# Squared-ReLU MLP of an encoder layer: the place of one PSUM copy on ScalarE, and the order of GpSimd's DMAs

## The chip, the cores and the metric

The kernel runs on one core of one Trainium2 chip. A core has engines that each work through their own list of instructions in order: TensorE (PE in the profile; its weight loads are listed apart as PEld), VectorE (DVE), ScalarE (ACT), GpSimd (POOL) and SyncE (SP). SP and GpSimd issue the transfers (DMAs) here. The engines meet through semaphores. TensorE writes PSUM, which is cut into banks of 128 rows by 512 floats.

The metric is the device time of one execution in microseconds (us), as the median of three runs. Beside it stands one execution with the profiler on, from which all rows here come.

## The reference

One layer of an encoder, float32, 512 tokens of width 1024. Ahead of the part that matters here run an attention branch, a gated linear recurrence and a cross attention to 256 memory tokens. What the change touches is the layer's MLP with a hidden width of 4096, and the norm behind it:

```python
u = rmsnorm(h, norm_ff_g[l]) @ w1[l]
h = h + jnp.square(jax.nn.relu(u)) @ w2[l]
...
return rmsnorm(h, final_norm_g)
```

## The kernel before

**Float32 out of three products.** TensorE multiplies in a shorter format. Each operand is split into a high part (`hi`, ScalarE's copy to that format, L181) and a low part (`lo`, VectorE's difference, L185), and each product is the sum of three matmuls: hi by hi, hi by lo, lo by hi (L1409 to L1411 in the up product, L1536 to L1538 in the down product). Weights are loaded raw (`wr`), and their parts are `wh` and `wl`; the letter `u` or `d` behind them says whether they belong to the up weight w1 or the down weight w2, then come the group and the product, so `whu24` is the high part for the up product of group 2, product 4.

**Seven products instead of eight.** The hidden width is worked in eight groups of 512 (`g` = 0 to 7). From group 2 on the up product of a group (`mlp_up7`) is a two-by-two block product with seven instead of eight block products (Strassen's scheme, in Winograd's form), in the order of `PRODUCTS`: 1, 5, 6, 2, 7, 3, 4. They go to three PSUM banks: U takes 1, 6, 7 and 4, one on top of the other; Y takes 5 and 3; V takes 2. Between products the running sums are moved. After product 1 ScalarE copies U to V (L1415). After product 5 it copies Y to an SBUF tile `y5` (L1418). After product 6 it copies U to Y (L1420). After product 7 VectorE reads U and adds `y5` (L1424), after product 3 it does so with Y (L1427), and after product 4 ScalarE reads U. The results are squared behind a ReLU (L1378, L1379) into tiles `sq`. The down product (`mlp_down`) uses the same seven products and runs one group behind: up group 3, then down group 2, and so on; the last two groups' down products run together.

**Sums of weight blocks.** Products 5, 6 and 7 need sums of weight blocks. These are made in DRAM by DMA ahead of time: SP copies a block to `wsu` or `wsd` (the copies in `sum_jobs`), and GpSimd issues a DMA that adds another block to it (L444). The class `Presum` paces these: `tick` counts TensorE's work in us as estimated from the matmuls' sizes, and whenever a due time has passed, `emit` takes the next addition and ties it to the matmul just traced. From 306 us of such work on, one falls due every 12.5 us (`PACE`). Product 4's weight block is not loaded. It is product 6's raw block, once that has been split, plus one more block, which GpSimd's DMA adds in place (L1350). So product 4's split (L181, L185) has to wait until this addition has landed, and the addition has to wait until VectorE has split product 6's block.

**What sets the order.** TensorE's list stands as it is written. The lists of the other engines are ordered by a scheduler ahead of time, from priorities (the order of the text, moved by `ahead`) and from its own idea of when each operand is there. `ahead(PW)`, with PW = -20, puts a split back by 20 places against the text around it. `tc.keep_in_program_order(i)` binds instruction `i` behind the instruction that was traced last before it on the same engine; it adds no wait on a semaphore. A call of `unit` runs the `prep` of all units up to three places behind the one asked for, so the split of product 4 is traced at the start of product 2, just behind the copy of U to Y; the scheduler's list has it ahead of that copy all the same.

**Buffers.** There are four buffers each for high and low parts, three PSUM banks for U and V and the up products of the first two groups, and five places in turn for raw blocks, so SP's loads and ScalarE's splits are released as TensorE and VectorE finish with earlier blocks.

Of the kernel before, what the change touches and what calls it, by code (L numbers as in the profile page):

```python
# [12 lines left out]
AF = mybir.ActivationFunctionType  # L13
ALU = mybir.AluOpType
# [18 lines left out]
P1, P2, P3, P4, PW = 20, 20, 20, 10, -20  # L33
# [9 lines left out]
PACE = (183.0, 5.1), (306.0, 12.5)  # L43
# [3 lines left out]
def emit(  # L47
# [22 lines left out]
    te, ve, ac, gp = nc.tensor, nc.vector, nc.scalar, nc.gpsimd  # L70
# [26 lines left out]
    def s4(shape, name, dt=F32):  # L97
        return s4p.tile([P] + shape, dt, tag="s4", name=name)

    def k4(shape, name, dt=F32):  # L100
        return k4p.tile([P] + shape, dt, tag="k4", name=name)
# [7 lines left out]
    def t2(name, dt=F32, shape=(S,)):  # L109
        return t2p.tile([P] + list(shape), dt, tag="t2", name=name)  # L110
# [6 lines left out]
    def mm(name, shape=(S,)):  # L117
        return mmp.tile([P] + list(shape), F32, tag="mm", name=name)
# [4 lines left out]
    def sc(name, shape=(S,)):  # L123
        return scp.tile([P] + list(shape), F32, tag="sc", name=name)
# [4 lines left out]
    def f(a):  # L129
        return a.bitcast(F32)  # L130
# [41 lines left out]
    def new_parts(shape, name):  # L172
        pad = [P, UK * (UW + FH)]
        hi = whp.tile([P, shape[0] * shape[1]], R, tag="wh", name=f"wh{name}", padded_shape=pad)
        lo = wlp.tile([P, shape[0] * shape[1]], R, tag="wl", name=f"wl{name}", padded_shape=pad)
        return [t.rearrange("p (k n) -> p k n", k=shape[0]) for t in (hi, lo)]

    def split_of(hi, lo, raw):
        def split(what="hl"):
            if "h" in what:  # L180
                ac.activation(hi, raw, AF.Copy)  # L181
            if "v" in what:
                ve.tensor_copy(hi, raw)
            if "l" in what:
                ve.tensor_tensor(lo, raw, f(hi), ALU.subtract)  # L185

        return split

# [99 lines left out]
    def ahead(n):  # L288

        return tc.high_priority(offset=n) if n else nullcontext()  # L290
# [157 lines left out]
    class Presum:  # L448
# [3 lines left out]
        def emit(self):  # L452
            while self.jobs:
                dma = next(self.jobs[0], None)
                if dma is None:
                    self.jobs.popleft()
                    continue
                sync = mybir.DependencyInfo(mybir.DependencyClass.Sync, mybir.DependencyReason.DATA)
                tc.add_manual_dep(dma.ins, self.at.ins.name, sync, reason="presum")
                if len(self.jobs) > 1:  # L460
                    self.jobs[0], self.jobs[1] = self.jobs[1], self.jobs[0]
                return dma
# [189 lines left out]
    for hp in range(2):  # L652
        wt = next_panel()
        for j in range(2):
            h = 2 * hp + j
            ps = mm(f"gq{h}")
# [124 lines left out]
    for li, m in enumerate(mlev):  # L781
# [8 lines left out]
        for hp in range(2):  # L790
# [3 lines left out]
            ps = sc(f"lv{hp}{m}", (NT, 2, w))  # L794
# [516 lines left out]
    def raw_tile(name):  # L1311
        raw_n[0] += 1
        if raw_n[0] % RAWS == 3:
            return t4(f"wr{name}")
        if raw_n[0] % RAWS in (0, 2):
            return wrp.tile([P, D], F32, tag="wr", name=f"wr{name}", padded_shape=[P, UK * UW])
        return s4([D], f"wr{name}")
# [3 lines left out]
    def add_unit(key, shape):  # L1321

        kind, g, part = key[:3]
        name = "".join(map(str, key))
        block = block1 if kind == "u" else block2
        box = []

        def load():
            if part == "4":
                box.append(raws.pop((kind, g)))  # L1330
                return
            if part == "6":
                raw = raws[kind, g] = s4(shape, f"wr{name}")
            else:
                raw = raw_tile(name).rearrange("p (k n) -> p k n", k=shape[0])
            if part in SUMS:
                src = wsum[kind, g, part]
            else:
                src = block(g, QUAD[part] if part in QUAD else f"{key[3]}{part}")
            nc.sync.dma_start(raw, src)  # L1340
            box.append(raw)

        def prep():
            while not box:
                load_q.popleft()()
            unit = new_parts(shape, name)
            with ahead(PW):
                split_of(unit[0], unit[1], box[0])()
            if part == "6":
                gp.dma_start(box[0], block(g, "10"), accum_op=ALU.add)  # L1350
            units[key] = unit

        unit_q.append((key, prep))
        load_q.append(load)

# [9 lines left out]
    def unit(*key):  # L1365

        while key not in units:
            unit_q.popleft()[1]()
        got = units[key]
        at = order.index(key)  # L1370
        while unit_q and len(order) - len(unit_q) < at + 4:
            unit_q.popleft()[1]()
        while load_q and len(order) - len(load_q) < at + LOADS:
            load_q.popleft()()
        return got

    def square(ps, out_, sign=1.0):
        ac.activation(out_, ps, AF.Relu, scale=sign)  # L1378
        ac.activation(out_, out_, AF.Square)  # L1379
# [10 lines left out]
    def mlp_up7(g):  # L1390

        qa, qb = (k4([2, S], f"sq{g}{j}") for j in range(2))
        sqs[g, 0], sqs[g, 1] = qa, qb
        h1, h2 = slice(0, HS), slice(HS, S)
        bank = {}

        for name in PRODUCTS:
            b = {"5": "Y", "3": "Y", "2": "V"}.get(name, "U")
            if b not in bank:
                bank[b] = (pvt if b == "Y" else mm)(f"u{b}{g}").rearrange("p (i n) -> p i n", i=2)  # L1400
                if b == "V":
                    pass
            ps = bank[b]
            whi, wlo = unit("u", g, name)
            xh, xl = xsum[name]
            for k in range(UK):
                for i in range(2):
                    ws, begin = slice(i * P, (i + 1) * P), name in "15" and k == 0 and i == 0
                    te.matmul(ps[:, i, :], whi[:, k, ws], xh[:, k, :], start=begin, stop=False, skip_group_check=True)  # L1409
                    te.matmul(ps[:, i, :], whi[:, k, ws], xl[:, k, :], start=False, stop=False, skip_group_check=True)  # L1410
                    at = te.matmul(ps[:, i, :], wlo[:, k, ws], xh[:, k, :], start=False, stop=k == UK - 1, skip_group_check=True)  # L1411
                presum.tick(6 * HS / 2400, at)
            if name == "1":
                bank["V"] = mm(f"uV{g}").rearrange("p (i n) -> p i n", i=2)
                ac.activation(bank["V"], ps, AF.Copy)  # L1415
            elif name == "5":
                y5 = t2(f"y5{g}", F32, (2, HS))
                ac.activation(y5, ps, AF.Copy)  # L1418
            elif name == "6":
                ac.activation(bank["Y"], ps, AF.Copy)  # L1420
            elif name == "2":
                square(ps, qa[:, :, h1])
            elif name == "7":
                ve.tensor_tensor(qb[:, :, h2], ps, y5, ALU.add)  # L1424
                square(qb[:, :, h2], qb[:, :, h2], -1.0)
            elif name == "3":
                ve.tensor_tensor(qb[:, :, h1], ps, y5, ALU.add)  # L1427
                square(qb[:, :, h1], qb[:, :, h1], -1.0)
            else:
                square(ps, qa[:, :, h2])  # L1430
            yield
# [222 lines left out]
    def mlp_up_group(g):  # L1654
        if g in SEVEN:
            yield from mlp_up7(g)
            return
        for j in range(2):
            if g < 2:
                wt = next_panel()  # L1660
                if (g, j) == (1, 1):
                    for _ in range(2):
                        unit_q.popleft()[1]()
            else:
                wt = tuple(list(x) for x in zip(*(unit("u", g, j, n) for n in range(2))))
            yield from mlp_up(g, j, wt)
# [64 lines left out]
```

## Time and profile before

| | us |
|---|---|
| median of three runs | 791.28 |
| the three runs | 789.46, 791.28, 793.39 |
| the profiled execution, its own time | 787.97 |
| its span, first to last instruction | 786.2 |
| TensorE busy | 755.5 |
| VectorE busy | 541.3 |
| ScalarE busy | 430.4 |

The up groups 2 to 7 with the down products between them take from 494 to 741 us of the span; behind them the last two groups' down products and the final norm are left. Rows of the waits read "engine line waited for: us in total, times, longest". Rows of a time line read "start, duration, engine, line, operation, what it writes and reads", with the idle time of the engine before it and what ended that in brackets. Rows of a view by stretches read "start:end, length", then the busy time of TensorE, its weight loads, VectorE, ScalarE and GpSimd with the number of instructions, then TensorE's granted clock as a share of full speed, the busy share of the DMA engines, and the GB/s moved.

### The profile page before, as it was taken

The numbers are of one execution on the slowest core, as the hardware profiler recorded it, in microseconds if no ns is written. First come the engines' busy times: TensorE is split into PE (matmuls) and PEld (weight loads), VectorE is DVE, ScalarE is ACT, GpSimd is POOL, SyncE is SP. The second block draws the span as 40 slices with busy tenths as digits, with TensorE's granted clock in tenths as the row PEclk, the third lists the DMA queues.
The fourth block names the chain that finished last, engine by engine and source line by source line (L and its number), as shares of the span: only waits on it lengthen the run. The fifth ranks groups of instructions, "written<-read, shape, count | busy, mean of one in ns | idle before, by whom it ended". The sixth has DMA issues, their size and how long they took to land.

```text
span 786.2 us, 11996 instructions
## 1 busy us (share of the span) xinstructions
PE 755.5 (96%) x4501; PEld 656.6 (84%) x4501; DVE 541.3 (69%) x844; ACT 430.4 (55%) x715; POOL 196.5 (25%) x274
## 2 busy tenths in 40 slices
PE   9999999999999999999999999899997979799896
PEld 6888888898889988888888888888897878799885
DVE  5647753678787577565555689677784948568597
ACT  6645535576576433254434866564845546364773
POOL 7216522513433067311121101111111101100024
PEclk9999999999999999999999999999998999989999
DMA  8552987658866789856677496978785868847442
GB/s 247 182 136 80 303 255 249 187 190 271 291 191 214 210 165 185 188 110 129 159 145 169 98 290 162 255 177 235 178 230 134 237 161 195 234 135 218 131 108 107
DMA packets 106619, 148.17 MB, mean 188 GB/s; under 512 B 6033, under 2 KB 73146, under 8 KB 106562
## 3 DMA queue, kind: packets, MB, share of 16 engines
q1 hardware_dynamic: 83826, 109.12, 43.1%
q0 software_dynamic: 22144, 37.25, 27.1%
q10 hardware_dynamic: 592, 1.05, 0.4%
q8 instruction: 35, 0.57, 0.3%
q14 instruction: 22, 0.18, 0.1%
HBM read 143.19 MB, written 48.25 MB: 244 GB/s over the span
## 4 chain that ended last, share of the span: by engine, by line
PE 66%; issue 21%; DMA 5%; POOL 3%; DVE 2%; ACT 2%; SPq 0%; POOLq 0%; ACTq 0%; DVEq 0%
DMA wru<-in_w_dram 4%; PE wo L253 2%; PE xw L255 2%; PE xw L254 2%; PE xw L253 2%; PE u L253 2%; PE wo L254 2%; PE u L254 2%; PE u L255 2%; PE wo L255 2%; PE xq L254 2%; PE xq L255 2%; PE xq L253 2%; PE U L1537 1%; PE pv L1060 1%
## 5 line engine op out<-in xcount | busy, mean ns | idle before, releaser
L181 ACT ACTIVATE whu<-wru 128x1024 fp32r<-128x1024 f32 x42 | 44.4, 1056 | 69.4 <-DMA wru<-in_w_dram 35.4
L185 DVE TENSOR_TENSOR wlu<-wru,whu 128x1024 fp32r<-128x1024 f32 x42 | 50.3, 1219 | 44.9 <-ACT whu L181 44.8
L185 DVE TENSOR_TENSOR wld<-wrd,whd 128x1024 fp32r<-128x1024 f32 x56 | 68.4, 1223 | 15.9 <-ACT whd L181 15.8
L181 ACT ACTIVATE whd<-wrd 128x1024 fp32r<-128x1024 f32 x56 | 59.0, 1054 | 22.2 <-PE uU L1410 11.9
L1409 PE MATMUL uU<-xs_hi,whu 128*128 128x256 f32 x96 | 31.3, 326 | 21.8 <-ACT uY L1420 21.8
L1536 PE MATMUL U<-whd,hb 128*128 128x512 f32 x120 | 46.8, 390 | 0.0
L1537 PE MATMUL U<-wld,hb 128*128 128x512 f32 x120 | 46.8, 390 | 0.0
L1538 PE MATMUL U<-whd,hb 128*128 128x512 f32 x120 | 46.7, 389 | 0.0
L444 POOL DMA_DIRECT2D wsd<-in_w_dram x16 | 17.0, 1060 | 110.1 <-PE uU L1411 25.9
L1409 PEld LDWEIGHTS uU<-xs_hi,whu 128*128 128x128 f32 x96 | 21.7, 226 | 23.0 <-ACT uY L1420 23.0
L1012 POOL TENSOR_SCALAR bi<-nF,Ft 128x128 f32<-128x128 f32 (+3 forms) x32 | 20.8, 657 | 60.4 <-PE pt L1044 35.2
L1350 POOL DMA_DIRECT2D wrd<-in_w_dram x8 | 9.6, 1198 | 93.6 <-DVE wld L185 93.6
L1410 PE MATMUL uU<-xs_lo,whu 128*128 128x256 f32 x96 | 30.5, 317 | 0.0
L1411 PE MATMUL uU<-xs_hi,wlu 128*128 128x256 f32 x96 | 30.4, 317 | 0.0
L444 POOL DMA_DIRECT2D wsu<-in_w_dram x12 | 14.1, 1177 | 62.7 <-PE xq L255 21.0
L1409 PE MATMUL uY<-xs_hi,whu 128*128 128x256 f32 x96 | 27.7, 288 | 0.0
L1410 PE MATMUL uY<-xs_lo,whu 128*128 128x256 f32 x96 | 27.5, 286 | 0.0
L1411 PE MATMUL uY<-xs_hi,wlu 128*128 128x256 f32 x96 | 27.4, 286 | 0.0
L1411 PE MATMUL uU<-x_hi,wlu 128*128 128x256 f32 x96 | 27.2, 283 | 0.0
L1410 PE MATMUL uU<-x_lo,whu 128*128 128x256 f32 x96 | 27.2, 283 | 0.0
L1409 PE MATMUL uU<-x_hi,whu 128*128 128x256 f32 x96 | 27.1, 283 | 0.0
L1155 ACT ACTIVATE x_hi<-hT,gv 128x512 fp32r<-128x512 f32 x16 | 11.5, 716 | 27.5 <-DVE hT L1154 27.4
(997 smaller groups left out, 2685.5 us busy)
## 6 DMA issues: line engine op xcount, KB each, us to landing
wsd<-in_w_dram SPq DMA_DIRECT2D x24, 512.0 KB, 5.4
wrd<-in_w_dram SPq DMA_DIRECT2D x24, 512.0 KB, 6.0
wrd<-wsd SPq DMA_DIRECT2D x24, 512.0 KB, 5.1
wsu<-in_w_dram SPq DMA_DIRECT2D x18, 512.0 KB, 7.7
wru<-in_w_dram SPq DMA_DIRECT2D x18, 512.0 KB, 4.9
wru<-wsu SPq DMA_DIRECT2D x18, 512.0 KB, 4.7
wsd<-in_w_dram POOLq DMA_DIRECT2D x16, 512.0 KB, 7.1
wsu<-in_w_dram POOLq DMA_DIRECT2D x12, 512.0 KB, 7.4
```

Of the source, the lines that this page charges most:

```text
L181: ac.activation(hi, raw, AF.Copy)
L185: ve.tensor_tensor(lo, raw, f(hi), ALU.subtract)
L253: te.matmul(ps, wh, hi, start=n_ == 0 and not begun, stop=False)
L254: te.matmul(ps, wh, lo, start=False, stop=False)
L255: at = te.matmul(ps, wl, hi, start=False, stop=k == order[-1])
L444: yield gp.dma_start(wsum[kind, g, name], src, accum_op=ALU.add, **more)
L1409: te.matmul(ps[:, i, :], whi[:, k, ws], xh[:, k, :], start=begin, stop=False, skip_group_check=True)
L1410: te.matmul(ps[:, i, :], whi[:, k, ws], xl[:, k, :], start=False, stop=False, skip_group_check=True)
L1411: at = te.matmul(ps[:, i, :], wlo[:, k, ws], xh[:, k, :], start=False, stop=k == UK - 1, skip_group_check=True)
L1536: te.matmul(ps, hi, whi[:, k, :], start=begin, stop=False, skip_group_check=True)
L1537: te.matmul(ps, hi, wlo[:, k, :], start=False, stop=False, skip_group_check=True)
L1538: at = te.matmul(ps, lo, whi[:, k, :], start=False, stop=k == 1, skip_group_check=True)
```

## The change

Two things are moved; no instruction is added or taken away.

On ScalarE the copy of U to Y after product 6 is bound behind what is traced ahead of it, and product 4's split in an up group loses its shift by `ahead` and is bound in the same way. The piece of ScalarE's list in group 2 shows it. `y52` is the copy of product 5, `hb12` a hidden block for the down product of group 1, `uY2` the copy of U to Y, `whd11` the first down split of group 1, `sq20` the squares of product 2. Before:

```order
L1418 ACTIVATE y52_5165<-uY2_5134 128x512
L1485 ACTIVATE hb12_5264<-sq11_4865 128x512
L181 ACTIVATE whu24_5198<-wru26_4988 128x1024
L1420 ACTIVATE uY2_5134<-uU2_5101 128x512
L181 ACTIVATE whd11_5231<-wrd11_5106 128x1024
L1378 ACTIVATE sq20_5099<-uV2_5132 128x2x256
L1379 ACTIVATE sq20_5099<-sq20_5099 128x2x256
```

The same piece after (the lines of the text have moved on by one to seven):

```order
L1425 ACTIVATE y52_5165<-uY2_5134 128x512
L1492 ACTIVATE hb12_5264<-sq11_4865 128x512
L1427 ACTIVATE uY2_5134<-uU2_5101 128x512
L182 ACTIVATE whu24_5198<-wru26_4988 128x1024
L182 ACTIVATE whd11_5231<-wrd11_5106 128x1024
L1385 ACTIVATE sq20_5099<-uV2_5132 128x2x256
L1386 ACTIVATE sq20_5099<-sq20_5099 128x2x256
```

The copy `uY2` and the split `whu24` have changed places. The same exchange stands in each of the groups 2 to 7, and nothing else on ScalarE has moved. The lists of TensorE, VectorE and SP are as before.

On GpSimd the additions into raw blocks (L1350) and, from 306 us of TensorE's work on, the paced additions (L444) are bound to the order of the text. `wru46`, `wru56` and `wru66` are the raw blocks of product 6 in the up groups 4, 5 and 6, onto which product 4's part is added; `wsu` and `wsd` are sums made ahead for later groups. Before:

```order
L444 DMA wsd56_225<-wsd55_223 256x512
L444 DMA wsu76_228<-wsu75_226 256x512
L1350 DMA wru46_5798<-in_w1_dram 128x4x256
L444 DMA wsd65_229<-in_w2_dram 256x1x512
L1350 DMA wrd36_5981<-in_w2_dram 128x2x512
L444 DMA wsd75_232<-in_w2_dram 256x1x512
L444 DMA wsd67_230<-in_w2_dram 256x1x512
L1350 DMA wru56_6202<-in_w1_dram 128x4x256
L444 DMA wsd77_233<-in_w2_dram 256x1x512
L1350 DMA wrd46_6386<-in_w2_dram 128x2x512
L444 DMA wsd66_231<-wsd65_229 256x512
L444 DMA wsd76_234<-wsd75_232 256x512
```

After:

```order
L446 DMA wsd56_225<-wsd55_223 256x512
L1357 DMA wru46_5798<-in_w1_dram 128x4x256
L446 DMA wsu76_228<-wsu75_226 256x512
L446 DMA wsd65_229<-in_w2_dram 256x1x512
L1357 DMA wrd36_5981<-in_w2_dram 128x2x512
L446 DMA wsd75_232<-in_w2_dram 256x1x512
L1357 DMA wru56_6202<-in_w1_dram 128x4x256
L446 DMA wsd67_230<-in_w2_dram 256x1x512
L446 DMA wsd77_233<-in_w2_dram 256x1x512
L1357 DMA wrd46_6386<-in_w2_dram 128x2x512
L446 DMA wsd66_231<-wsd65_229 256x512
L1357 DMA wru66_6607<-in_w1_dram 128x4x256
```

Three pairs have changed places: `wru46` now stands ahead of `wsu76`, `wru56` ahead of `wsd67`, and `wru66` ahead of `wsd76`, which follows right behind the last row. In groups 2, 3 and 7 GpSimd's list is as it was. The diff:

```diff
     def split_of(hi, lo, raw):
         def split(what="hl"):
+            at = None
             if "h" in what:
-                ac.activation(hi, raw, AF.Copy)
+                at = ac.activation(hi, raw, AF.Copy)
...
+            return at
...
                 tc.add_manual_dep(dma.ins, self.at.ins.name, sync, reason="presum")
+                if self.spent >= PACE[-1][0]:
+                    tc.keep_in_program_order(dma)
...
             unit = new_parts(shape, name)
-            with ahead(PW):
-                split_of(unit[0], unit[1], box[0])()
+            late = (kind, part) == ("u", "4")
+            with ahead(0 if late else PW):
+                split = split_of(unit[0], unit[1], box[0])()
+                if late:
+                    tc.keep_in_program_order(split)
             if part == "6":
-                gp.dma_start(box[0], block(g, "10"), accum_op=ALU.add)
+                tc.keep_in_program_order(gp.dma_start(box[0], block(g, "10"), accum_op=ALU.add))
...
             elif name == "6":
-                ac.activation(bank["Y"], ps, AF.Copy)
+                tc.keep_in_program_order(ac.activation(bank["Y"], ps, AF.Copy))
```

## The prediction

> **What bounds the kernel now.** I read the page's busy shares first, then the waits of TensorE, then the time line around the waits that are left.
>
> ```profile
> PE 755.5 (96%) x4501; PEld 656.6 (84%) x4501; DVE 541.3 (69%) x844; ACT 430.4 (55%) x715; POOL 196.5 (25%) x274
> PE uU L1409 <- ACT uY L1420: 21.8, 6, 5.0
> PE warm L365 <- DVE ones L369: 1.3, 1, 1.3
> ACT whu L181 <- DMA wru<-in_w_dram: 35.4, 6, 7.2
> ```
>
> TensorE is busy for 96% of the span. In its list of waits one stands out: six times, once in each up group of seven products, it waits for ScalarE's copy of bank U to Y (L1420), 21.8 us in all. Nothing behind it comes near (1.3 us at the start). ScalarE's own list gives the reason: it waits six times for a DMA into `wru`, 35.4 us in all. The time line of ScalarE in group 2 shows how the two hang together.
>
> ```profile
> 506.19 1.06 ACT L181 ACTIVATE whu<-wru 128x1024 fp32r<-128x1024 f32 x1 [4.41 <-DMA wru<-in_w_dram]
> 507.15 0.58 ACT L1420 ACTIVATE uY<-uU 128x512 f32<-128x512 f32 x1
> 507.67 1.04 ACT L181 ACTIVATE whd<-wrd 128x1024 fp32r<-128x1024 f32 x1
> 508.61 0.57 ACT L1378 ACTIVATE sq<-uV 128x512 f32<-128x512 f32 x1
> 510.00 0.63 ACT L1485 ACTIVATE hb<-s 128x512 fp32r<-128x512 f32 x1
> ```
>
> The first row is product 4's split. Its raw block is product 6's, onto which GpSimd's DMA has to add another block first. ScalarE works in order, so the copy of U, whose input was ready, stands behind a split that waits 4.41 us for that landing. Product 7 writes U and can't begin before the copy has read it:
>
> ```profile
> 502.52 0.28 PE L1409 MATMUL uV<-x_hi,whu 128*128 128x256 f32 x1
> 505.28 0.28 PE L1411 MATMUL uV<-x_hi,wlu 128*128 128x256 f32 x1
> 507.79 0.39 PE L1409 MATMUL uU<-xs_hi,whu 128*128 128x256 f32 x1 [2.23 <-ACT uY L1420]
> ...
> 551.59 0.39 PE L1409 MATMUL uU<-xs_hi,whu 128*128 128x256 f32 x1 [2.85 <-ACT uY L1420]
> 595.33 0.58 PE L1409 MATMUL uU<-xs_hi,whu 128*128 128x256 f32 x1 [4.27 <-ACT uY L1420]
> 642.51 0.58 PE L1409 MATMUL uU<-xs_hi,whu 128*128 128x256 f32 x1 [5.00 <-ACT uY L1420]
> 688.39 0.58 PE L1409 MATMUL uU<-xs_hi,whu 128*128 128x256 f32 x1 [4.94 <-ACT uY L1420]
> 732.69 0.39 PE L1409 MATMUL uU<-xs_hi,whu 128*128 128x256 f32 x1 [2.52 <-ACT uY L1420]
> ```
>
> The first two rows are the first and the last of product 2's 24 matmuls: they start 0.12 apart, so a product takes 24 x 0.12 = 2.88 us. The six bracketed waits count from a matmul's modelled end (0.28 after its start), while the next could have started 0.12 after it. Each delay is therefore 0.16 longer: 21.8 + 6 x 0.16 = 22.8 us.
>
> The waits cost a second time. The view by stretches shows the granted clock:
>
> ```profile
> 509.40:512.70 3.30, 3.30 (x18) 3.30 (x17) 1.88 (x3) 1.92 (x3) 0.00 (x0) 0.50 0.58 161
> 539.90:582.30 42.40, 39.55 (x255) 36.05 (x254) 32.00 (x40) 25.57 (x34) 5.54 (x5) 1.00 0.83 208
> 594.70:601.40 6.70, 6.08 (x28) 6.08 (x29) 3.69 (x4) 4.05 (x7) 1.08 (x1) 0.50 0.42 93
> 642.50:645.80 3.30, 3.29 (x15) 3.30 (x16) 2.37 (x3) 2.67 (x4) 0.00 (x0) 0.50 0.38 100
> 686.90:693.60 6.70, 5.21 (x24) 5.21 (x25) 3.14 (x3) 4.15 (x6) 0.00 (x0) 0.50 0.28 81
> 721.40:738.60 17.20, 14.68 (x123) 14.47 (x122) 8.52 (x8) 9.65 (x13) 1.30 (x1) 1.00 0.56 144
> ```
>
> The third number from the end is the clock. Right after four of the six waits it is 0.50 for 3.3 or 6.7 us; after those of 2.85 and 2.52 us it stays 1.00. In the four stretches TensorE is busy 3.30 + 6.08 + 3.29 + 5.21 = 17.9 us at half speed, so 8.9 us are lost. What the six waits cost today is 22.8 + 8.9 = 31.7 us.
>
> [...]
>
> **The change, part by part.** *The copy ahead of the split.* No instruction is added or removed. ScalarE does `uY` as soon as product 6 is done and its 0.58 us ends before product 2 does, so the wait before product 7 goes: 31.7 us. The split isn't delayed by it, since it waits for its landing anyway; it and all behind it on ScalarE come 507.67 - 507.15 = 0.52 us earlier against the landing.
>
> What is late next is bank U once more, one step on. Product 4 adds onto U after product 7, and VectorE must read U in between (L1424). On VectorE that read stands behind the low parts of two splits and of a hidden block, which wait for ScalarE's rows above. So the landing now works through to product 4. Group 3, where this chain wasn't held up by product 7, prices it:
>
> ```profile
> 549.99 1.06 ACT L181 ACTIVATE whu<-wru 128x1024 fp32r<-128x1024 f32 x1 [5.03 <-DMA wru<-in_w_dram]
> 593.73 1.06 ACT L181 ACTIVATE whu<-wru 128x1024 fp32r<-128x1024 f32 x1 [6.45 <-DMA wru<-in_w_dram]
> 640.91 1.06 ACT L181 ACTIVATE whu<-wru 128x1024 fp32r<-128x1024 f32 x1 [7.18 <-DMA wru<-in_w_dram]
> 686.79 1.06 ACT L181 ACTIVATE whu<-wru 128x1024 fp32r<-128x1024 f32 x1 [7.12 <-DMA wru<-in_w_dram]
> 731.09 1.06 ACT L181 ACTIVATE whu<-wru 128x1024 fp32r<-128x1024 f32 x1 [5.22 <-DMA wru<-in_w_dram]
> 555.07 0.68 DVE L1424 TENSOR_TENSOR sq<-uU,y 128x512 f32<-128x512 f32 x1
> ```
>
> From the split's start to the read's end are 555.07 + 0.68 - 549.99 = 5.76 us; without the copy in between 5.24, and about 0.1 until TensorE starts (an estimate: in group 2 product 7 starts 0.06 after the copy's end). Unhindered, product 7 could begin at its wait's end minus the wait minus 0.16: 505.40 in group 2, then 548.58, 590.90, 637.35, 683.29 and 730.01. Product 4 could begin two products, 5.76 us, after that. So a wait of (split's start - product 7's unhindered start) + 5.34 - 5.76 remains: 0.37 in group 2, 0.99 in group 3, 0.66 in group 7. For the others it needs the second part.
>
> *GpSimd's order.* From group 4 on the addition into `wru` is issued ahead of a sum that stood before it. This moves three DMAs (`wsu76`, `wsd67`, `wsd76`), each by one place.
>
> ```profile
> 497.24 1.32 POOL L1350 DMA_DIRECT2D wru<-in_w_dram  x1 [6.09 <-DVE wlu L185]
> 541.73 1.33 POOL L1350 DMA_DIRECT2D wru<-in_w_dram  x1 [5.88 <-DVE wlu L185]
> 578.50 0.88 POOL L444 DMA_DIRECT2D wsu<-wsu  x1 [11.29 <-PE U L1538]
> 583.16 1.35 POOL L1350 DMA_DIRECT2D wru<-in_w_dram  x1 [3.78 <-DVE wlu L185]
> 627.01 1.03 POOL L444 DMA_DIRECT2D wsd<-in_w_dram  x1 [11.89 <-PE uU L1411]
> 629.60 1.33 POOL L1350 DMA_DIRECT2D wru<-in_w_dram  x1 [1.56 <-DVE wlu L185]
> 675.12 0.89 POOL L444 DMA_DIRECT2D wsd<-wsd  x1 [12.80 <-PE uU L1411]
> 675.69 1.67 POOL L1350 DMA_DIRECT2D wru<-in_w_dram  x1
> 721.91 1.30 POOL L1350 DMA_DIRECT2D wru<-in_w_dram  x1 [21.50 <-DVE wlu L185]
> ```
>
> From these issues to the splits' starts it is 8.95 us in group 2, 8.26 in 3 and 9.18 in 7, where no sum stands close ahead, but 10.57, 11.31 and 11.10 in groups 4, 5 and 6, where one does. I take the mean of the first three, 8.80, for the three groups. Their splits then start at 591.96, 638.40 and 684.49, and waits of 0.64, 0.63 and 0.78 remain. The bounds are 8.26 (0.1 each) and no gain at all (2.41, 3.14 and 3.08). The three sums wait for VectorE's split with the addition, up to 583.16 - 578.50 = 4.7 us longer, and land that much later. Nothing needs them soon: they feed loads of group 6's or 7's blocks, tens of microseconds on, so I cost this at nothing; the cover is the distance of a group.
>
> *The sum.* 0.37 + 0.99 + 0.64 + 0.63 + 0.78 + 0.66 = 4.1 us of new waits, all too short for the half clock by the rows above. The gain is 31.7 - 4.1 = 27.6 us. The profiled execution took 787.97 us by its own time (span 786.2), so 760.4. It was 3.3 us faster than the median of the runs, 791.28, which by the same gain comes to 763.7. The runs spread over 789.46 to 793.39; since TensorE waits for hardly anything but these landings, part of that spread should be theirs and go with them. I take 762.0.
>
> **The rivals.** *The additions don't land earlier.* The DMA share is 0.83 in the second stretch above, so the loads of SP's queue, and not the sum ahead, may hold the additions up. [...] Then the waits before product 4 are 0.37 + 0.99 + 2.41 + 3.14 + 3.08 + 0.66 = 10.7 us and the gain is 21.0: 767 to 770.3. Three waits of 2.4 to 3.1 us may each bring 3.4 us of half clock, 1.7 lost, so up to 775.4. Against it: all three long landings are just those with a sum ahead.
>
> *The loads crowd.* With 28 us less the same transfers come in a shorter time: 0.83 x 42.4 = 35.2 us of them in a group of 42.4 - 3.0 + 0.7 = 40.1 us, a share of 0.88. If each landing is 1.5 us later for it, the waits grow by 9 us: 769.4 to 772.7. For it speaks the 0.83, against it that loads are released by work that follows TensorE and so move with it.
>
> *Slower.* The same mechanism decides the sign if it is strong. A group loses 31.7 / 6 = 5.3 us now; it loses more once the landing is 0.42 + 5.3 = 5.7 us behind product 7's unhindered start. Now the mean is (0.79 + 1.41 + 2.83 + 3.56 + 3.50 + 1.08) / 6 = 2.2, so each landing would have to be 3.5 us later than today. At 5.5 us later the waits are 6 x (2.2 + 5.5 - 0.42) = 44 us, 12 more than now, and the time is 800 to 803. No landing of the trace takes that long.
>
> *It does nothing:* something else would have to hold the copy or product 7 as long. The copy needs only product 6, whose matmuls are all issued ahead of product 2's first row at 502.52, and TensorE's list names no other release for product 7. This has next to no weight.
>
> **How the numbers follow.** The forecast holds 0.70 (757 to 767 of its own), additions not earlier 0.17, crowding 0.07, slower 0.04, no change 0.02. Half a per cent, 4 us, is about what a measurement of this kernel can tell from no change. All but the last two are faster by more: 0.94; same 0.02; slower 0.04. The range begins where nearly nothing of the loss remains (787.97 - 31.7 = 756.3) and takes in most of the first two rivals: 756.5 to 773.
>
> **What would show it.** ScalarE's copy `uY` starts about 0.1 us after product 6 ends, in all six groups, and TensorE has no wait before product 7. TensorE's waits are then before product 4, for VectorE's read of U, under 1 us each. The issue to landing of the additions in groups 4 to 6 falls to 8 to 9 us. No half clock stands between 500 us and the end of the MLP, and a group takes some 40 us. The forecast is wrong if landings stay at 11 us, if waits of over 2 us stand before product 4, or if a load from SP's queue becomes what a split waits for.

## The result, and the profile after

The changed kernel takes 763.02 us (median of six runs, 761.76 to 765.28), the kernel before beside it 792.76 us (six runs, 789.46 to 793.79). The ratio is 0.9635, with a 95% interval of 0.9612 to 0.9659. The forecast was 762.0, in a range of 756.5 to 773.

The profiled execution of the changed kernel took 765.28 us by its own time (span 763.4). It is the slowest of the six, while the profiled execution before, at 787.97, was faster than all six of its own. So between the two profiles there are 22.7 us, between the medians 29.7.

The busy times of the engines, from the page of the kernel after:

```profile
PE 749.3 (98%) x4501; PEld 650.7 (85%) x4501; DVE 539.2 (71%) x844; ACT 429.3 (56%) x715; POOL 196.9 (26%) x274
```

Its waits of TensorE and of ScalarE:

```profile
PE uU L1416 <- DVE sq L1431: 5.4, 6, 2.4
PE warm L367 <- DVE ones L371: 1.3, 1, 1.3
```

```profile
ACT whu L182 <- DMA wru<-in_w_dram: 19.9, 6, 4.7
```

The wait for the copy of U (21.8 us) is gone from TensorE's list. In its place stands a wait of 5.4 us in six pieces for VectorE's read of U, which product 4 needs. ScalarE waits 19.9 instead of 35.4 us for the landings. The time line of ScalarE in group 2 and, below the dots, of product 4's split in groups 3 to 7:

```profile
503.05 0.58 ACT L1427 ACTIVATE uY<-uU 128x512 f32<-128x512 f32 x1 [1.00 <-PE uU L1418]
506.92 1.06 ACT L182 ACTIVATE whu<-wru 128x1024 fp32r<-128x1024 f32 x1 [3.28 <-DMA wru<-in_w_dram]
507.88 1.04 ACT L182 ACTIVATE whd<-wrd 128x1024 fp32r<-128x1024 f32 x1
510.40 0.63 ACT L1492 ACTIVATE hb<-s 128x512 fp32r<-128x512 f32 x1 [0.33 <-DVE wld L186]
...
548.72 1.06 ACT L182 ACTIVATE whu<-wru 128x1024 fp32r<-128x1024 f32 x1 [4.73 <-DMA wru<-in_w_dram]
589.89 1.06 ACT L182 ACTIVATE whu<-wru 128x1024 fp32r<-128x1024 f32 x1 [2.61 <-DMA wru<-in_w_dram]
629.58 1.06 ACT L182 ACTIVATE whu<-wru 128x1024 fp32r<-128x1024 f32 x1 [2.61 <-DMA wru<-in_w_dram]
669.25 1.06 ACT L182 ACTIVATE whu<-wru 128x1024 fp32r<-128x1024 f32 x1 [2.60 <-DMA wru<-in_w_dram]
710.42 1.06 ACT L182 ACTIVATE whu<-wru 128x1024 fp32r<-128x1024 f32 x1 [4.09 <-DMA wru<-in_w_dram]
```

The copy now stands ahead of the split that waits. TensorE's time line shows product 6's last matmul, product 2's first, and product 4's first in the six groups:

```profile
502.67 0.28 PE L1418 MATMUL uU<-xs_hi,wlu 128*128 128x256 f32 x1
502.79 0.28 PE L1416 MATMUL uV<-x_hi,whu 128*128 128x256 f32 x1
...
512.51 0.36 PE L1416 MATMUL uU<-x_hi,whu 128*128 128x256 f32 x1 [0.91 <-DVE sq L1431]
554.31 0.36 PE L1416 MATMUL uU<-x_hi,whu 128*128 128x256 f32 x1 [2.36 <-DVE sq L1431]
595.48 0.35 PE L1416 MATMUL uU<-x_hi,whu 128*128 128x256 f32 x1 [0.24 <-DVE sq L1431]
635.17 0.36 PE L1416 MATMUL uU<-x_hi,whu 128*128 128x256 f32 x1 [0.25 <-DVE sq L1431]
674.84 0.36 PE L1416 MATMUL uU<-x_hi,whu 128*128 128x256 f32 x1 [0.23 <-DVE sq L1431]
715.71 0.36 PE L1416 MATMUL uU<-x_hi,whu 128*128 128x256 f32 x1 [1.42 <-DVE sq L1431]
```

Product 6 ends at 502.67 + 0.28 = 502.95, and the copy starts at 503.05, 0.10 us later, as the forecast said; in the five other groups the trace has the same 0.10. The waits are 0.9, 2.4, three times about 0.24, and 1.4 us. With 0.16 added to each, as before, the delays are 1.07, 2.52, 0.40, 0.41, 0.39 and 1.58, together 6.4 us. Of the half-clock stretches in the MLP one is left, behind the longest of these waits. In the view by stretches the clock is again the third number from the end; the first stretch lies right behind that wait, the two others are free of it:

```profile
555.30:558.60 3.30, 3.30 (x18) 3.30 (x17) 1.82 (x2) 2.29 (x4) 0.61 (x1) 0.50 0.46 159
580.70:617.00 36.30, 36.06 (x228) 32.71 (x227) 28.15 (x36) 24.19 (x33) 5.67 (x5) 1.00 0.87 213
674.90:714.00 39.10, 39.10 (x251) 35.81 (x252) 28.96 (x35) 22.85 (x31) 2.52 (x2) 1.00 0.65 189
```

It costs 3.30 / 2 = 1.65 us, so what is left of the landings' price in this execution is 6.4 + 1.65 = 8.0 us. GpSimd's time line shows the issues of the six additions, in group 3 the sum that stands ahead, and in group 4 the sum that now stands behind:

```profile
497.51 1.32 POOL L1357 DMA_DIRECT2D wru<-in_w_dram  x1 [6.08 <-DVE wlu L186]
532.27 1.04 POOL L446 DMA_DIRECT2D wsd<-in_w_dram  x1 [12.43 <-PE Y L1545]
539.26 1.33 POOL L1357 DMA_DIRECT2D wru<-in_w_dram  x1 [5.95 <-DVE wlu L186]
581.59 1.32 POOL L1357 DMA_DIRECT2D wru<-in_w_dram  x1 [15.96 <-DVE wlu L186]
582.38 1.53 POOL L446 DMA_DIRECT2D wsu<-wsu  x1
621.34 1.32 POOL L1357 DMA_DIRECT2D wru<-in_w_dram  x1 [14.56 <-DVE wlu L186]
661.03 1.32 POOL L1357 DMA_DIRECT2D wru<-in_w_dram  x1 [13.33 <-DVE wlu L186]
700.34 1.30 POOL L1357 DMA_DIRECT2D wru<-in_w_dram  x1 [20.60 <-DVE wlu L186]
```

From issue to the split's start it is 9.41, 9.46, 8.30, 8.24, 8.22 and 10.08 us in groups 2 to 7. In groups 4, 5 and 6 that is 2.3, 3.1 and 2.9 less than before. In groups 2, 3 and 7, where GpSimd's list is unchanged, it is 0.5, 1.2 and 0.9 more. (The landing itself comes up to 0.1 us ahead of the split's start; where landing times stand below, they are the transfer's own.)

### The profile page after: what moved, and what is told of

The parts are those of the page before. It is cut to its first block, busy times and chain, and to the rows that moved or that the text cites. A ratio compares the mean times of both kernels' runs of the same rounds, so it can differ in the third digit from the quotient of the medians.

```text
span 763.4 us, 11997 instructions
## 1 busy us (share of the span) xinstructions
PE 749.3 (98%) x4501; PEld 650.7 (85%) x4501; DVE 539.2 (71%) x844; ACT 429.3 (56%) x715; POOL 196.9 (26%) x274
## 4 chain that ended last, share of the span: by engine, by line
PE 67%; issue 14%; DMA 9%; ACT 4%; DVE 4%; POOL 1%; SPq 0%; POOLq 0%; ACTq 0%; DVEq 0%
DMA wru<-in_w_dram 6%; DMA wru<-wsu 3%; PE wo L255 2%; PE xw L255 2%; PE xw L257 2%; PE xw L256 2%; PE wo L256 2%; PE u L257 2%; PE u L256 2%; PE u L255 2%; PE wo L257 2%; PE xq L256 2%; PE xq L257 2%; PE xq L255 2%; PE U L1544 1%
## 5 line engine op out<-in xcount | busy, mean ns | idle before, releaser
L182 ACT ACTIVATE whu<-wru 128x1024 fp32r<-128x1024 f32 x42 | 44.4, 1057 | 53.9 <-DMA wru<-in_w_dram 19.9
L1357 POOL DMA_DIRECT2D wru<-in_w_dram x6 | 7.9, 1322 | 76.5 <-DVE wlu L186 76.5
L1416 PE MATMUL uU<-xs_hi,whu 128*128 128x256 f32 x96 | 27.2, 283 | 0.0
L1417 PE MATMUL uU<-xs_lo,whu 128*128 128x256 f32 x96 | 27.2, 283 | 0.0
L1418 PE MATMUL uU<-xs_hi,wlu 128*128 128x256 f32 x96 | 27.2, 283 | 0.0
```

The lines of the kernel that those rows point to most:

```text
L182: at = ac.activation(hi, raw, AF.Copy)
```

## The experiments

Theory: the copy's place removes the wait before product 7, GpSimd's order shortens three landings, each part is worth something by itself, and what is left are waits for the read of U. The rivals: the landings are late because of SP's loads and GpSimd's order is worth nothing; or the chain to product 4 is too long even without a late landing. Each kernel ran four times beside runs of the kernel before on the same chip: seven of 791.73 us median (786.92 to 796.63) beside the first four kernels, seven of 789.84 (786.06 to 793.00) beside the last three.

**ScalarE's part alone.** The changed kernel with GpSimd's list as it was before:

```diff
-                if self.spent >= PACE[-1][0]:
-                    tc.keep_in_program_order(dma)
...
-                tc.keep_in_program_order(gp.dma_start(box[0], block(g, "10"), accum_op=ALU.add))
+                gp.dma_start(box[0], block(g, "10"), accum_op=ALU.add)
```

> ScalarE's copy ahead of product 4's split, GpSimd's list as before the change. If a sum that stands ahead in GpSimd's list is what makes the additions of groups 4 to 6 land late, they take 10.5 to 11.3 us again (8.2 to 8.3 with the change), TensorE waits 2.6 to 3.4 us before product 4 in each of these groups in place of 0.4, and with up to three half clocks of some 1.6 us the time is 771 to 776 us. If the order of GpSimd's list doesn't matter and the copy is the whole gain, it is 763 us and the additions land after 8.3 us all the same.

Measured: 775.17 us (773.38 to 776.24), ratio 0.9793 (0.9742 to 0.9845). From its waits of TensorE:

```profile
PE uU L1414 <- DVE sq L1429: 13.5, 6, 5.0
```

The time is in the expected range; the waits in groups 4, 5 and 6 are 2.4, 2.1 and 5.0 us where 2.6 to 3.4 were expected. The longest is in group 6. GpSimd's and ScalarE's time lines there, and TensorE's in groups 4 to 6:

```profile
666.37 0.89 POOL L446 DMA_DIRECT2D wsd<-wsd  x1 [12.80 <-PE uU L1416]
666.94 1.67 POOL L1355 DMA_DIRECT2D wru<-in_w_dram  x1
```

```profile
679.83 1.06 ACT L182 ACTIVATE whu<-wru 128x1024 fp32r<-128x1024 f32 x1 [7.33 <-DMA wru<-in_w_dram]
```

```profile
597.98 0.36 PE L1414 MATMUL uU<-x_hi,whu 128*128 128x256 f32 x1 [2.38 <-DVE sq L1429]
639.54 0.35 PE L1414 MATMUL uU<-x_hi,whu 128*128 128x256 f32 x1 [2.12 <-DVE sq L1429]
685.42 0.55 PE L1414 MATMUL uU<-x_hi,whu 128*128 128x256 f32 x1 [4.95 <-DVE sq L1429]
```

With the sum issued 0.57 us ahead, the addition takes 679.83 - 666.94 = 12.9 us to the split's start, and TensorE waits 4.95 us for what hangs on it. In this profile the six landings take 10.8, 8.3, 10.4, 10.1, 12.9 and 9.2 us, and three half-clock stretches follow (from 514.3, 640.6 and 684.9 us). The lists of all engines but GpSimd are those of the changed kernel, and in groups 4 to 6 all three landings are longer than the 8.2 to 8.3 us there. So the sum ahead does cost landing time, and the rival of the loads alone is refuted.

This run also shows what ScalarE's part is worth. Before, product 7 starts 1.60 us after the split's start (507.79 - 506.19 in group 2); after the change product 4, which comes two products (5.76 us together) later, starts 5.59 us after it (512.51 - 506.92). A landing may thus come 1.60 + 5.76 - 5.59 = 1.77 us later than before for the same delay. The part doesn't cut TensorE loose from the landing; it moves the deadline, by 6 x 1.77 = 10.6 us over the six groups.

**GpSimd's part alone.** The kernel before with those two bindings only.

```diff
+                if self.spent >= PACE[-1][0]:
+                    tc.keep_in_program_order(dma)
...
-                gp.dma_start(box[0], block(g, "10"), accum_op=ALU.add)
+                tc.keep_in_program_order(gp.dma_start(box[0], block(g, "10"), accum_op=ALU.add))
```

> GpSimd's list as in the change, ScalarE's copy behind the split as before. If the landing sets the wait before product 7, the landings of groups 4 to 6 come 2.3 to 3.0 us earlier, TensorE's waits there fall from 4.3, 5.0 and 4.9 to about 2.1 us each, some of the half clocks go with them, and the time is 776 to 785 us. If the order of GpSimd's list doesn't matter, it is 792 us as before.

Measured: 777.84 us (777.40 to 779.53), ratio 0.9827 (0.9768 to 0.9887). Its waits of TensorE and of ScalarE:

```profile
PE uU L1411 <- ACT uY L1422: 14.9, 6, 3.7
```

```profile
ACT whu L181 <- DMA wru<-in_w_dram: 28.5, 6, 5.9
```

The wait for the copy is still there but shorter. TensorE's time line in groups 4, 5 and 6:

```profile
596.88 0.38 PE L1411 MATMUL uU<-xs_hi,whu 128*128 128x256 f32 x1 [2.19 <-ACT uY L1422]
639.86 0.39 PE L1411 MATMUL uU<-xs_hi,whu 128*128 128x256 f32 x1 [2.02 <-ACT uY L1422]
681.35 0.39 PE L1411 MATMUL uU<-xs_hi,whu 128*128 128x256 f32 x1 [2.01 <-ACT uY L1422]
```

The waits are 2.2, 2.0 and 2.0 us instead of 4.27, 5.00 and 4.94, and the landings there take 8.41, 8.24 and 8.22 us. Four half-clock stretches of 3.4 us are left (from 509.0, 553.4, 597.8 and 724.1 us). By the medians the parts alone gain 16.6 and 13.9 us, together 30.5; the change as a whole gained 29.7, and 27.8 when it was run once more (the last experiment). They add up within what the runs can tell.

**VectorE's read ahead of the low parts.** The changed kernel, with VectorE's read of U after product 7 put ahead of the low parts of product 4's split and of the first down split (whose high parts ScalarE still makes in the order of the change):

```diff
+                after7 = late or key in lows_late
...
-                split = split_of(unit[0], unit[1], box[0])()
+                split = split_of(unit[0], unit[1], box[0])
+                at = split("h" if after7 else "hl")
...
+                if after7:
+                    lows.append(split)
...
                 ve.tensor_tensor(qb[:, :, h2], ps, y5, ALU.add)
+                for low in lows:
+                    tc.keep_in_program_order(low("l"))
+                lows.clear()
```

> The change, and VectorE reads bank U for product 7 ahead of the low parts of product 4's split and of the first down split, which are written behind it. If the waits left before product 4 (5.4 us and one half clock in the profile) come from this read standing behind work that waits for the landing, they vanish, and product 4 waits for its own split alone, which is in time: 755 to 758 us, and the runs lie closer together than the 3.5 us of the change. If the late low parts delay product 4 or the down products instead, the waits move there and the time is 763 us or more.

Measured: 760.29 us (759.51 to 762.21), ratio 0.9611 (0.9561 to 0.9661), 2.3 us above the expectation. Its waits of TensorE and, in group 7, VectorE's time line:

```profile
PE uU L1421 <- DVE sq L1436: 1.4, 1, 1.4
...
PE uU L1423 <- DVE wlu L186: 0.6, 1, 0.6
```

```profile
708.08 0.69 DVE L1504 TENSOR_TENSOR hb<-sq,hb 128x512 fp32r<-128x512 f32 x1 [9.19 <-ACT hb L1500]
708.69 0.69 DVE L1436 TENSOR_TENSOR sq<-uU,y 128x512 f32<-128x512 f32 x1
```

The waits went in groups 2 to 6; both rows are group 7's. The scheduler moved more than the read there: the hidden block of the down product went back on ScalarE (in group 4 it starts 6.1 us behind product 4's split, 3.5 in the changed kernel), and its low part with it on VectorE, so the gain belongs to the new order of both lists. In group 7 the read still stood behind something that hangs on the landing: the low part of a hidden block, whose high part is queued on ScalarE behind the waiting split. VectorE idled 9.19 us ahead of it. The expectation had overlooked that group 7's list differs.

**No additions.** The changed kernel without the six additions into product 6's raw blocks of the up weight:

```diff
-            if part == "6":
+            if part == "6" and kind == "d":
                 tc.keep_in_program_order(gp.dma_start(box[0], block(g, "10"), accum_op=ALU.add))
```

> The change without the six additions into the up groups' raw blocks: product 4 is computed from product 6's block, so the up groups' sums lack one weight block, and 6 transfers of 0.5 MB are gone. If the landing is behind all of TensorE's waits in the MLP, they vanish: 755 to 758 us, as with the read ahead. If the chain of ScalarE and VectorE between the split and the read of U is too long by itself, waits of 0.4 us and more stay before product 4 in every group and the time is 760 to 763 us.

Measured: 756.75 us (756.45 to 756.92), ratio 0.9562 (0.9514 to 0.9610). Its waits of TensorE begin so, and hold nothing of the MLP:

```profile
PE warm L367 <- DVE ones L371: 1.3, 1, 1.3
PE pt L1048 <- DVE bi L1040: 0.7, 1, 0.7
```

All other lists are those of the changed kernel. So the chain from the split to product 4 costs nothing when the split isn't late, and what the changed kernel still loses here hangs on the six additions. That rival is refuted too.

**The read ahead in group 7 as well.** The kernel with VectorE's read ahead of the low parts, and the low part of that hidden block in group 7 bound behind the read as well:

```diff
-                ve.tensor_tensor(qb[:, :, h2], ps, y5, ALU.add)
+                reads.append(ve.tensor_tensor(qb[:, :, h2], ps, y5, ALU.add))
...
-            ve.tensor_tensor(hb[:, 1], src, f(hb[:, 0]), ALU.subtract)
+            low = ve.tensor_tensor(hb[:, 1], src, f(hb[:, 0]), ALU.subtract)
+            if (g, name) == (NG - 1, "1"):
+                behind = mybir.DependencyInfo(mybir.DependencyClass.NoSync, mybir.DependencyReason.DATA)
+                tc.add_manual_dep(low.ins, reads[-1].ins.name, behind, reason="read first")
```

> The kernel with the read ahead, with one low part more (hidden block 7, product 1) put behind VectorE's read of bank U in group 7, where it stood ahead of it and TensorE waited 1.4 us for the read and 0.6 us for product 4's low part. If these two waits are what kept the read ahead from the 756.8 us without any addition, they go and the time is 757 to 758.5 us. If the order of the last down products is the rest, which has also moved, it stays at 760 us.

Measured: 757.52 us (757.27 to 758.04), ratio 0.9592 (0.9555 to 0.9629), as expected, and 4.5 us less than the changed kernel on the same chip (762.02, the last experiment). ScalarE's wait for the landings, and three stretches from 500 us to the end of the last up group:

```profile
ACT whu L182 <- DMA wru<-in_w_dram: 26.6, 6, 5.0
```

```profile
500.00:550.00 50.00, 50.00 (x345) 46.71 (x344) 34.97 (x44) 30.18 (x41) 6.99 (x6) 1.00 0.92 224
550.00:700.00 150.00, 150.00 (x951) 136.30 (x950) 122.65 (x152) 95.92 (x132) 18.26 (x16) 1.00 0.83 222
700.00:741.00 41.00, 41.00 (x226) 35.80 (x225) 33.32 (x40) 28.89 (x44) 7.22 (x7) 1.00 0.46 116
```

ScalarE waits longer for the landings than in the changed kernel (26.6 against 19.9 us), and the landings take 8.5 to 9.2 us, but TensorE is busy in every microsecond of the three stretches at full clock. This is the time without the landings' price for the sums further below.

**The read ahead, GpSimd's list as before.** The same kernel without the two bindings on GpSimd (the diff of the first experiment).

> The same kernel with GpSimd's list as before the change. With the read ahead, product 4 needs only its own two splits, some 2.4 us behind the landing, so a landing up to 3.3 us behind product 7's unhindered start costs nothing. The additions of groups 4 to 6 land after 10 to 13 us again (3 to 6 us behind that start), so waits of 0 to 2.5 us come back in one or two of these groups: 757 to 762 us, where the copy alone took 775. If the order of GpSimd's list mattered by itself and not through the read, the loss would be 12 us again, near 769.

Measured: 762.54 us (761.27 to 764.84), ratio 0.9658 (0.9617 to 0.9699), 0.5 us above the expectation. Its two longest waits of TensorE in the MLP:

```profile
PE uU L1421 <- DVE wlu L186: 1.2, 2, 0.8
...
PE uU L1419 <- ACT whu L182: 0.5, 1, 0.5
```

All other engines' lists are those of the kernel above. With the later deadline GpSimd's order is worth 5.0 us (762.54 - 757.52) instead of the 12.2 between the changed kernel and ScalarE's part alone (775.17 - 763.02). In groups 4, 5 and 6 the landings take 9.5, 10.4 and 11.3 us here, and now product 4 waits for its own operands. The listed waits are 1.7 of the 3.85 us between the two profiled executions (761.89 and 758.04). Laid beside the kernel above matmul by matmul, product 4 of groups 5 and 6 comes 2.3 us later by them, and four short waits in the down products of these groups (two of them for a hidden block from ScalarE) add 1.4. A further 0.55 us falls into the first 7 us of the program and about as much is regained behind the last matmul.

**The changed kernel once more,** beside the two kernels above and without an edit.

> The changed kernel itself, beside the other two on the same chip: 762 to 765 us, so that a difference of 4 to 6 us to the read ahead can be told from the scatter of the calls. The waits before product 4 and the half clock differ from profile to profile, since they follow the landings.

Measured: 762.02 us (760.54 to 763.34), ratio 0.9654 (0.9609 to 0.9699). The profiled execution is now the fastest of its four. Its wait before product 4:

```profile
PE uU L1416 <- DVE sq L1431: 2.6, 5, 0.9
```

That is less than half of the 5.4 us of the first profile, by the same list of instructions. Its landings take 9.12, 8.02, 8.25, 8.32, 8.33 and 8.44 us, with no half clock in the MLP: groups 3 and 7 came 1.4 and 1.6 us earlier.

## Why the prediction came out right

**The copy's place.** Right, with its two signs: the copy follows product 6 by 0.10 us, and no wait before product 7 is left. The price put on the six waits, 31.7 us, can be tested by the kernel in which TensorE doesn't wait: 757.5 + 31.7 = 789.2, against 787.97 measured for the profiled execution before, 1.2 us off.

**The next wait.** Right in its place: bank U, VectorE's read, product 4. It was mis-sized in the profiled execution, 8.0 us instead of 4.1. The sign "under 1 us each" failed there in groups 3 and 7 (2.36 and 1.42 us), and the wait in group 3 is one "of over 2 us before product 4", which the prediction had named as a sign of being wrong. In the repeated run no wait is over 0.95 us. The parts can be told:

| term | predicted | measured | adds, us |
|---|---|---|---|
| chain, split's start to product 4 | 5.34 | 5.59 in groups 2 to 6, 5.29 in 7 | +1.2 |
| landings of groups 4 to 6 | 8.80 | 8.30, 8.24, 8.22 | -1.6 |
| landings of groups 2, 3, 7 | 8.95, 8.26, 9.18 | 9.41, 9.46, 10.08 | +2.6 |
| half clock | none | one stretch | +1.65 |

The terms give 4.1 + 1.2 - 1.6 + 2.6 + 1.65 = 7.95. The chain is longer since it runs through VectorE's two low parts: without the copy ScalarE's second split starts 0.52 us earlier against the first, as the prediction had it, but the two low parts end only 0.3 earlier, and the hidden block on ScalarE now waits 0.33 us for them (the row at 510.40). At its lower bound the prediction's "0.1 each" should be 0.10, 0.09 and 0.24 by its own rows; nothing hangs on it.

The landings of groups 2, 3 and 7 were carried over from one execution as if they were constants. The repeated kernel gives 9.12, 8.02 and 8.44 for them; they scatter by over a microsecond from execution to execution. For group 3 the prediction's premise is also wrong: a sum does stand ahead of its addition, issued 7 us before it (the row at 532.27), and it lands at 541.74, 2.5 us after the addition's issue. Before the change that sum had 1.7 us left, and the addition took 8.2 us to land instead of 9.4; over the eight profiles with additions it took 8.0 to 9.4 us. In group 7 GpSimd has issued nothing for 21 us ahead of the addition. The busy share of the DMA engines doesn't explain its later landing: from issue to landing it was 0.98 before, where the landing took 9.09 us, and 0.86 after, where it took 9.99. What makes them scatter stays open.

The sum closes for both profiles of the change, within half a microsecond: 757.5 + 8.0 = 765.5 for the first (765.28 measured), and 757.5 + 2.6 + 5 x 0.16 = 760.9 for the second (760.54). With 1.65 us for each half-clock stretch it also fits the two parts alone: 757.5 + 13.5 + 6 x 0.16 + 3 x 1.65 = 776.9 (776.24), and 757.5 + 14.9 + 6 x 0.16 + 4 x 1.65 = 780.0 (779.53).

**No half clock.** The step "all too short for the half clock" failed once: product 4 of group 3, whose delay the sum had at 0.99 us, came 2.52 us late (a wait of 2.36), and a stretch at 0.50 followed. The prediction's rows had waits of this size with both outcomes (a half clock behind 2.23 us, none behind 2.85 and 2.52 us); the last section shows how these waits lay.

**GpSimd's order.** Right, and the size was underrated: landings 8.2 to 8.3 us instead of 8.80, and 1.2 us of delay in the three groups together instead of 2.05. The three sums put behind cost nothing that the profile shows, as forecast: TensorE's list of waits between 494 us and the end of the MLP holds nothing but the six waits above.

**The rivals.** "The additions don't land earlier" gave 767 to 775.4; the landings refute it, and the time of ScalarE's part alone (775.17) is what it would have given. "The loads crowd" fell too: the DMA share is 0.87 from 580.70 to 617.00, near the 0.88 that rival worked out, and just there the landing took 8.30 us. The longer landings of groups 2, 3 and 7 in the first profile were not the rule either: in the second, at a still shorter time, groups 3 and 7 came earlier than before the change. The other two had no part in it.

**The spread.** That part of the runs' spread is the landings' was assumed, and the runs agree: kernels in which TensorE waits on landings spread by 2 to 10 us (786.92 to 796.63 before, 760.54 to 763.34 for the change), the two without such waits by 0.5 and 0.8. So a forecast from one execution was bound to carry an error of a few microseconds. The forecast is 1.0 us below the median because it stands between its two sums (760.4 and 763.7), and the second was the better one. That it came so close is in part luck: the sizes were off by 3.9 us in one profile of the change, and the median before moved by 1.5 us (791.28 to 792.76) with three more runs.

## What to carry to other kernels

A ready copy that stands on an in-order engine behind an instruction that waits for a DMA passed that DMA's lateness on here (in group 2 ScalarE waited 4.41 us and TensorE 2.23 us behind it); putting the copy ahead moves the deadline to the next reader in the chain, so follow the chain to that reader, price how much later it may come, and see whether it can be moved too (here: 21.8 us of waits, then 5.4, then none once VectorE's read stood ahead of the low parts). Where a list differs in the first or last group, follow the chain there apart. A landing time from one execution is a sample (that of group 7 took 7.9 to 10.0 us in eight profiles): take it as a range, and look at a wait-free version to learn what the landings cost in all.

## What the runs showed of the hardware

**Where the half clock stood.** In the MLP of the kernel before, TensorE's granted clock is 0.50 from 509.35 to 512.76, 594.68 to 601.51, 642.47 to 645.88 and 686.84 to 693.67 us, 3.41 or 6.83 us each. The later starts lie 85.33, 133.12 and 177.49 us behind the first: 25, 39 and 52 times 3.413. In ScalarE's part alone the stretches start at 514.3, 640.6 and 684.9, 37 and 50 such lengths behind the first. Why they lie so is not shown.

With the MLP in the profiles of the kernel before and the changed kernel laid off in steps of that length from such a start, one can measure how much of TensorE's idle time falls into each step. The steps at full clock with a half clock behind them held 1.86, 3.41, 3.42 and 3.39 us of it before and 2.36 us after; all other steps at full clock held up to 1.58 us before and 1.41 us after. Two steps that were themselves at half clock (from 594.68 and 686.84 us in the kernel before) were followed by another with only 0.64 and 1.55 us idle; why is not shown. In these profiles the place of a wait counted, not its length alone. The waits of 2.85 and 2.52 us in the kernel before fall into two steps each (1.58 and 1.28, 1.04 and 1.48 us), that of 2.23 us has 1.86 us in one. In the rows of ScalarE's part alone above, the wait of 2.38 us that ends at 597.98 lies across a border of the steps (596.2), with about 1.8 us behind it, and no half clock follows; that of 2.12 us that ends at 639.54 lies within one step (637.2 to 640.6), and the stretch behind it runs at 0.50:

```profile
640.60:643.90 3.30, 3.30 (x18) 3.30 (x17) 1.75 (x2) 2.22 (x4) 0.68 (x1) 0.50 0.99 316
```

No run moved a wait within a step by itself, so this is what these profiles have in common, not a tested cause.

**A landing behind another sum.** From its issue an addition onto product 6's raw block took 7.9 to 10.8 us to land where the last transfer ahead on GpSimd's queue had been issued 6.9 us or more before (39 cases in the profiles, half of them up to 8.8), and 9.5 to 12.9 where a sum had been issued 0.6 to 5.5 us before (nine cases). In the kernel before, that sum still had 4.4, 5.8 and 5.5 us to its own landing when the additions of groups 4, 5 and 6 were issued, and these took 10.5, 11.2 and 11.0 us. A sum issued 0.8 us behind (the row at 582.38) left it at 8.30. That the order on the queue is a cause is shown by the kernels that differ in it alone (8.2 to 8.3 us in groups 4 to 6 of the changed kernel, 10.1 to 12.9 in ScalarE's part alone); that the time left is the measure is seen in these three cases and was not tested by itself.
